# A decoder block on one core: the third and fourth group of 512 hidden columns computed as one more Strassen block

## The chip, the cores and the metric

The kernel runs as one program on 1 core of a Trainium2 chip. The metric is the device time of one execution in microseconds (us). Of several timed executions the median is given; the trace comes from one profiled execution and is read with times from the start of its span.

## The reference, cut to what matters

One decoder layer on x (512 positions, width 2048, float32): an attention half and a recurrent half behind one input projection, an output projection, and then the feed-forward part, which is all that the change concerns:

```
h2 = rms_norm(x, norm2_w) * (1 + scale2) + shift2
ff = square(relu(h2 @ w_ff1)) @ w_ff2          # w_ff1 2048 x 8192, w_ff2 8192 x 2048
x  = x + gate2 * ff
```

Everything is float32. A product of two float32 matrices is made of three TensorE products: each operand is split into a rounded high part and the rest (hi and lo), and hi*hi, hi*lo and lo*hi are added up in PSUM.

## The kernel before, in words

The 8192 hidden columns are 16 groups of 512 (`NG`). The first `PLAIN` = 4 groups are computed plainly, one after the other, by `hidden(g)` (the first of them by `first_hidden`, which also finishes the normalisation). A plain group takes 16 steps of 128 rows of `w_ff1`; each step loads a piece of the weight (`wraw`, L192), casts it to `whi` on ScalarE (L39), takes `wlo` on VectorE (L40) and runs 4 column blocks x 3 matmuls of 128x512 (`ch_mm`, L209 to L211): 192 matmuls a group. The result stands with channels in the partitions, as the second product wants it.

The other 12 groups are computed two at a time, as 6 blocks of 1024 columns, by Strassen's scheme with 7 half-size products instead of 8. A product (`product`, L1183) goes through four pieces of the contraction, u = 0 to 3, 12 matmuls each, so 48 a product and 336 a block. The result of a block has positions in the partitions, so it is turned by TensorE (`turn`, L1225), 32 transposes of 128x128 a block, in two halves.

What a product needs:

- **Weights.** 16 raw pieces a block (`raw`, L1155, 512 KB each, issued by SyncE). VectorE makes the sums and differences that products 5, 6, 7 and 4 want in place (L1163); ScalarE casts each piece to `vhi` (L1179), VectorE takes `vlo` (L1180). A product has its own piece 0, 1, 2, 3 of both.
- **Inputs.** Products 4 and 2 use the halves of h2 that are in SBUF. Products 1, 3, 5, 6 and 7 read the *forms* of h2 (sums of its quarters, hi and lo) from DRAM tensors `h_hid` and `h_lod`: for each half of the contraction (u = 0, 1 and u = 2, 3) one load of `Fh` and one of `Fl` (L1141, 512 KB each, issued by GpSimdE's queue, POOL). Four buffers of each kind exist.

The forms are made once, by `input_forms(u)` for u = 0 to 3: VectorE forms the four sums in `xf` (L1080 to L1083), then two casts to a staging tile `part` on ScalarE and two remainders on VectorE (L1042, L1043) are written to DRAM by POOL (L1046). There are 5 staging tiles and one `xf`, shared with `make_forms`, which does the same for each finished hidden group (`f_hid`, `f_lod`, the operands of the second product). These four generators are put into `tasks` behind group 0 and advanced by one step at each of 12 places of `hidden(1)` (`tick`, L1017), so all of them are recorded within group 1. Groups 2 and 3 then find the list empty.

The first Strassen block takes its products in the order 1, 3, 5, 6, 7, 4, 2; the others in 1, 5, 6, 7, 3, 4, 2. Products 1 and 5 of a block are copied from PSUM to SBUF on ScalarE (L1238).

The order of TensorE's work is the order of the program (manual schedule); the order on the other engines and queues is made by a scheduler when the kernel is built. Each queue then works strictly in that order: an instruction that waits holds up all behind it on its engine.

The part of the program that steps from the plain groups to the blocks:

```
for item, following in zip(items, items[1:] + [None]):
    ...
    call = part_of(following) if following else None
    if stage_ == 1:
        banks, ahead = product(i, hparts, 0, ws, "bg" if first and j < 2 else "mm", False, call)
```

`items` begins with block `PLAIN // 2`, and `call` makes the weight pieces of the following product while the present one runs.

Of the kernel before, what the change touches and what calls it, by code (L numbers as in the profile page):

```python
# [44 lines left out]
def hybrid_block(ctx, tc, x, c, positions, norm1_w, w_ada, b_ada, w_in, q_norm_w, k_norm_w,  # L45
# [922 lines left out]
    def first_hidden():  # L968

        banks = [bank("f1") for _ in range(4)]  # L970
        accs = [gv.tile([P, 512], F32, name="acc") for _ in range(2)]
        rbc = gv.tile([P, 512], F32, name="rbc", bufs=1)
        raws = []
        for k0 in range(0, NK, 2):
            for j, (whi, wlo) in enumerate(load_w(ff1_v, k0, 0, 512, None, raws=raws)):
                k = k0 + j
                if k >= 12:
                    h2[k] = pair(k)
                    split_to(h2[k], uT[k])
                ch_mm(banks, *h2[k], whi, wlo, k == 0, k == NK - 1)  # L980
                if k < 2:
                    dve.tensor_scalar(accs[k], raws[j], s2c[:, k:k + 1], None, op0=ALU.mult)
                else:
                    dve.scalar_tensor_tensor(accs[k % 2], raws[j], s2c[:, k:k + 1], accs[k % 2], op0=ALU.mult, op1=ALU.add)
                if 2 <= k < 8:
                    tick()
                if k == 8:
                    pr = bank("prow", tag="mm")
                    for ti in range(NT):
                        pe.transpose(pr[:, ti * P:(ti + 1) * P], r2[:, ti:ti + 1].broadcast_to([P, P]), ident)  # L990
                    act.copy(rbc, pr)
                if k >= 8:
                    for i in range((k - 8) * 2, (k - 8) * 2 + 2):
                        if i <= k:
                            h2_finish(i, rbc)
        bias = sm2
        run_all(to_cols(accs, bias))
        for j in range(4):
            r = xr.tile([P, 512], F32, name="relu", tag="x")
            dve.tensor_tensor(r, banks[j], rbc, op=ALU.mult)  # L1000
            act.activation(r, r, AF.Relu, bias=bias[:, j:j + 1])
            yield r
# [7 lines left out]
    def hidden(g):  # L1010
        banks = [bank("f1", tag="mm" if g % 2 else "bg") for _ in range(4)]
        for k0 in range(0, NK, 2):
            for j, (whi, wlo) in enumerate(load_w(ff1_v, k0, g * 512)):
                k = k0 + j
                ch_mm(banks, *h2[k], whi, wlo, k == 0, k == NK - 1)
                if 2 <= k < 14:
                    tick()  # L1017
        for j in range(4):
            r = xr.tile([P, 512], F32, name="relu", tag="x")
            act.activation(r, banks[j], AF.Relu)  # L1020
            yield r
# [4 lines left out]

    NG = FF // 512
    FORMS = 7
    PLAIN = 4
    KG = 4  # L1030

    def forms_in_dram(name, n, forms=FORMS):
# [59 lines left out]
    st_ = ctx.enter_context(ExitStack())  # L1092
    for g in range(PLAIN):
        rs = list(hidden(g) if g else first_hidden())
# [51 lines left out]
    def weights(view, g0, c0, order):  # L1146


        w = {}
        second = ((1, 1), (0, 1)) if order[1] == 3 else ((0, 1), (1, 1))  # L1150
        with tc.high_priority():
            for e, n in ((0, 0), *second, (1, 0)):
                for u in range(KG):
                    w[u, e, n] = raw = pools[f"raw{e + 1}{n + 1}"].tile([P, 2, 512], F32, name="raw2")
                    nc.sync.dma_start(raw, view[:, g0 + u, e, :, c0 + n * 512:c0 + (n + 1) * 512])  # L1155
        return w
# [161 lines left out]
    def part_of(item):  # L1318

        stage_, blk, j, i = item  # L1320
        if j == 0:
            part_of.w = weights(ff1_s, 0, blk * 1024, order_of(item)) if stage_ == 1 else \
                weights(ff2_s, blk[1] * KG, blk[0] * 1024, order)
        w, first = part_of.w, blk == PLAIN // 2

# [5 lines left out]
    def order_of(item):  # L1331
        return first_order if item[1] == PLAIN // 2 else order

    items = [(1, b, j, i) for b in range(PLAIN // 2, NG // 2) for j, i in enumerate(order_of((1, b)))]
    items += [(2, (q, c), j, i) for q in range(2) for c in range(NC) for j, i in enumerate(order)]
# [5 lines left out]
    for item, following in zip(items, items[1:] + [None]):  # L1341
        stage_, blk, j, i = item
        first = blk == PLAIN // 2
        if j == 0 and stage_ == 1 and not first:
# [75 lines left out]
def _program(arrays):  # L1420
    import concourse.bacc as bacc
    nc = bacc.Bacc("TRN2", target_bir_lowering=False, num_devices=1)
    args = [nc.dram_tensor(n, a.shape, mybir.dt.from_np(a.dtype), kind="ExternalInput").ap()
            for n, a in arrays.items()]
    args.append(nc.dram_tensor("out_0_dram", _OUTS[0][0], F32, kind="ExternalOutput").ap())
    with tile.TileContext(nc, schedule_with_timeline_sim=True) as tc:
        hybrid_block(tc, *args)
    return nc
# [10 lines left out]
```

## Time and profile before

| | |
|---|---|
| median of 3 runs | 2274.7 us (2272.88 to 2276.16) |
| profiled execution | 2273.89 us, span 2272.1 us |
| granted TensorE clock | 0.998 of full |
| TensorE matmul | 2219.7 us, 98% of the span |
| VectorE | 1809.6 us, 80% |
| ScalarE | 1097.3 us, 48% |
| GpSimdE | 441.8 us, 19% |
| DMA | 598.32 MB, mean 263 GB/s |

In the rows of the profile, PE is TensorE's matmul, PEld its weight load, DVE is VectorE, ACT ScalarE, POOL GpSimdE (its rows here are DMA issues), SP SyncE. A row names the line, the engine, the operation and `out<-in`. An interval in brackets is idle time just before the instruction and what ended it. Matmuls are pipelined: one lasts 0.39 us, but the next starts 0.227 us after it.

### The profile page before, as it was taken

The numbers are of one execution on the slowest core, as the hardware profiler recorded it, in microseconds if no ns is written. First come the engines' busy times: TensorE is split into PE (matmuls) and PEld (weight loads), VectorE is DVE, ScalarE is ACT, GpSimd is POOL, SyncE is SP. The second block draws the span as 40 slices with busy tenths as digits, with TensorE's granted clock in tenths as the row PEclk, the third lists the DMA queues.
The fourth block names the chain that finished last, engine by engine and source line by source line (L and its number), as shares of the span: only waits on it lengthen the run. The fifth ranks groups of instructions, "written<-read, shape, count | busy, mean of one in ns | idle before, by whom it ended". The sixth has DMA issues, their size and how long they took to land.

```text
span 2272.1 us, 33110 instructions
## 1 busy us (share of the span) xinstructions
PE 2219.7 (98%) x11769; PEld 1821.1 (80%) x11769; DVE 1809.6 (80%) x2765; ACT 1097.3 (48%) x1950; POOL 441.8 (19%) x664
## 2 busy tenths in 40 slices
PE   4899999999999999999999999999999999999999
PEld 3788778888778888888887888888888888888887
DVE  6999878768786575678658988998897779967878
ACT  5555434443454464457544555565564333443332
POOL 1000022000220000003232323323232222222221
PEclk9999999999999999999999999999999999999999
DMA  9799454646555266747879789879889987998884
GB/s 324 255 335 336 139 177 150 214 149 211 170 178 160 71 227 202 267 120 264 322 280 361 274 306 385 297 290 377 319 294 378 358 310 263 349 347 310 305 295 164
DMA packets 262583, 598.32 MB, mean 263 GB/s; under 512 B 23220, under 2 KB 43968, under 8 KB 262416
## 3 DMA queue, kind: packets, MB, share of 16 engines
q1 hardware_dynamic: 186800, 332.54, 43.6%
q0 software_dynamic: 70720, 254.21, 30.4%
q10 hardware_dynamic: 4896, 9.44, 1.2%
q8 instruction: 93, 1.52, 0.3%
q14 instruction: 74, 0.61, 0.1%
HBM read 518.49 MB, written 77.61 MB: 262 GB/s over the span
## 4 chain that ended last, share of the span: by engine, by line
PE 70%; DMA 10%; DVE 8%; issue 8%; POOL 2%; ACT 1%; SPq 0%; POOLq 0%; DVEq 0%; ACTq 0%
PE f L1197 9%; PE f L1196 9%; PE f L1195 9%; PE prj L201 8%; PE prj L203 8%; PE prj L202 8%; DMA araw<-in_w_ada_dram 3%; PE f L211 2%; PE f L209 2%; PE f L210 2%; DVE vlo L1180 2%; DMA f_lod<-fs 2%; DVE raw L1163 2%; PE prj L209 1%; PE prj L210 1%
## 5 line engine op out<-in xcount | busy, mean ns | idle before, releaser
L1179 ACT CAST vhi<-raw 128x1024 fp32r<-128x1024 f32 x392 | 413.5, 1055 | 534.1 <-PE f L1197 419.4
L1180 DVE TENSOR_TENSOR vlo<-raw,vhi 128x1024 fp32r<-128x1024 f32 x392 | 476.3, 1221 | 150.8 <-ACT vhi L1179 150.0
L1196 PE MATMUL f<-vlo,Fh 128*128 128x512 f32 x1376 | 537.1, 390 | 3.4 <-DVE vlo L1180 3.3
L1197 PE MATMUL f<-vhi,Fl 128*128 128x512 f32 x1376 | 535.8, 389 | 0.5 <-DMA Fl<-f_lod 0.5
L1195 PE MATMUL f<-vhi,Fh 128*128 128x512 f32 x1376 | 536.1, 390 | 0.0
L39 ACT CAST whi<-wraw 128x512 fp32r<-128x512 f32 (+1 forms) x368 | 219.8, 601 | 445.9 <-PE prj L203 309.7
L201 PE MATMUL prj<-whi,hi 128*128 128x512 f32 x896 | 363.5, 406 | 1.3 <-ACT gg L711 1.3
L203 PE MATMUL prj<-whi,lo 128*128 128x512 f32 x896 | 350.6, 391 | 0.0
L202 PE MATMUL prj<-wlo,hi 128*128 128x512 f32 x896 | 350.0, 391 | 0.6 <-DVE wlo L40 0.6
L40 DVE TENSOR_TENSOR wlo<-wraw,whi 128x512 fp32r<-128x512 f32 (+1 forms) x368 | 243.3, 666 | 115.3 <-ACT whi L39 109.5
L131 DVE SCALAR_TENSOR_TENSOR acc<-araw,sc,acc 128x512 f32<-128x512 f32 (+1 forms) x392 | 254.0, 674 | 99.8 <-DMA araw<-in_w_ada_dram 98.6
L1196 PEld LDWEIGHTS f<-vlo,Fh 128*128 128x128 f32 x1376 | 258.3, 188 | 62.3 <-DVE vlo L1180 8.9
L1197 PEld LDWEIGHTS f<-vhi,Fl 128*128 128x128 f32 x1376 | 258.3, 188 | 54.2 <-DMA Fl<-f_lod 0.9
L1195 PEld LDWEIGHTS f<-vhi,Fh 128*128 128x128 f32 x1376 | 258.3, 188 | 53.7
L1163 DVE TENSOR_TENSOR raw<-raw,raw 128x1024 f32<-128x1024 f32 x224 | 268.3, 1218 | 3.5 <-DMA raw<-in_w_ff_dram 3.1
L203 PEld LDWEIGHTS prj<-whi,lo 128*128 128x128 f32 x896 | 168.1, 188 | 36.6 <-DVE lo L243 0.3
L201 PEld LDWEIGHTS prj<-whi,hi 128*128 128x128 f32 x896 | 168.3, 188 | 36.4 <-ACT gg L711 1.6
L202 PEld LDWEIGHTS prj<-wlo,hi 128*128 128x128 f32 x896 | 168.6, 188 | 33.5 <-DVE wlo L40 1.7
L1141 POOL DMA_DIRECT2D Fh<-f_hid x112 | 79.0, 705 | 424.0 <-PE f L1197 410.3
L211 PE MATMUL f<-hi,wlo 128*128 128x512 f32 x256 | 99.9, 390 | 1.2 <-DVE wlo L40 1.2
L209 PE MATMUL f<-hi,whi 128*128 128x512 f32 x256 | 100.3, 392 | 0.0
L210 PE MATMUL f<-lo,whi 128*128 128x512 f32 x256 | 99.6, 389 | 0.0
(311 smaller groups left out, 2912.0 us busy)
## 6 DMA issues: line engine op xcount, KB each, us to landing
raw<-in_w_ff_dram SPq DMA_DIRECT2D x224, 512.0 KB, 10.1
araw<-in_w_ada_dram SPq DMA_DIRECT2D x384, 256.0 KB, 4.3
Fh<-f_hid POOLq DMA_DIRECT2D x112, 512.0 KB, 6.7
Fl<-f_lod POOLq DMA_DIRECT2D x112, 512.0 KB, 7.8
wraw<-in_w_in_dram SPq DMA_DIRECT2D x104, 512.0 KB, 4.4
Fh<-h_hid POOLq DMA_DIRECT2D x60, 512.0 KB, 6.4
Fl<-h_lod POOLq DMA_DIRECT2D x60, 512.0 KB, 7.4
f_hid<-part POOLq DMA_DIRECT2D x48, 512.0 KB, 8.0
```

What stands on the lines that cost most here:

```text
L39: nc.scalar.copy(hi, src)
L40: (eng or nc.vector).tensor_tensor(lo, src, hi.bitcast(F32), op=ALU.subtract)
L131: dve.scalar_tensor_tensor(acc, raw[:, k - k0], vec[:, k:k + 1], acc, op0=ALU.mult, op1=ALU.add)
L201: pe.matmul(banks[ti], lhsT=hi[:, ts], rhs=whi, start=first, stop=False)
L202: pe.matmul(banks[ti], lhsT=hi[:, ts], rhs=wlo, start=False, stop=False)
L203: pe.matmul(banks[ti], lhsT=lo[:, ts], rhs=whi, start=False, stop=last)
L1163: dve.tensor_tensor(dst, a, b, op=ALU.subtract)
L1179: cast_done.append(act.copy(hi, src))
L1180: split_done.append(dve.tensor_tensor(lo, src, hi.bitcast(F32), op=ALU.subtract))
L1195: pe.matmul(banks[t], lhsT=fh[u][a][:, ts], rhs=whi[:, a], start=first, stop=False)
L1196: pe.matmul(banks[t], lhsT=fh[u][a][:, ts], rhs=wlo[:, a], start=False, stop=False)
L1197: pe.matmul(banks[t], lhsT=fl[u][a][:, ts], rhs=whi[:, a], start=False, stop=end)
```

## The change

One number changes:

```
@@ -1026,7 +1026,7 @@
     NG = FF // 512
     FORMS = 7
-    PLAIN = 4
+    PLAIN = 2
     KG = 4
```

The loop over plain groups ends after groups 0 and 1. `items` begins at block 1 instead of block 2, so there are 7 Strassen blocks, and the *first* block (order 1, 3, 5, 6, 7, 4, 2) now follows group 1 directly. The making of the forms stays in `hidden(1)`.

The scheduler orders the queues anew. In the following lists the number behind a name tells buffers apart.

**POOL, from the end of the forms of u = 1 on.** `part_11234` and `part_11235` are the second pair of forms (slots 6 and 7) of u = 1, `part_11287` to `part_11316` belong to u = 2, `part_11368` to `part_11387` to u = 3. Before:

```order
L1046 DMA h_hid_10581<-part_11234 128x2x512
L1046 DMA h_lod_10582<-part_11217 128x2x512
L1046 DMA h_lod_10582<-part_11235 128x2x512
L1046 DMA h_hid_10581<-part_11287 128x2x512
L1046 DMA h_lod_10582<-part_11288 128x2x512
L1046 DMA h_hid_10581<-part_11315 128x2x512
L1046 DMA h_lod_10582<-part_11316 128x2x512
L1046 DMA h_hid_10581<-part_11368 128x2x512
L1046 DMA h_lod_10582<-part_11369 128x2x512
L1046 DMA h_hid_10581<-part_11386 128x2x512
```

Now the loads of product 1 (`Fh_11572` to `Fl_11578`) and the first one of product 3 (`Fh_11648`) stand among them:

```order
L1046 DMA h_lod_10582<-part_11235 128x2x512
L1141 DMA Fh_11572<-h_hid_10581 128x2x512
L1141 DMA Fl_11574<-h_lod_10582 128x2x512
L1141 DMA Fh_11576<-h_hid_10581 128x2x512
L1141 DMA Fl_11578<-h_lod_10582 128x2x512
L1141 DMA Fh_11648<-h_hid_10581 128x2x512
L1046 DMA h_hid_10581<-part_11287 128x2x512
L1046 DMA h_lod_10582<-part_11288 128x2x512
L1046 DMA h_hid_10581<-part_11315 128x2x512
L1141 DMA Fl_11650<-h_lod_10582 128x2x512
L1046 DMA h_lod_10582<-part_11316 128x2x512
L1046 DMA h_hid_10581<-part_11368 128x2x512
```

The loads of the first block have moved from behind all writes of forms to a place between them; the writes of u = 2 and 3 stand behind the loads of product 1.

**POOL, the inputs of products 1 and 3.** Before, the first block's loads stood together: `Fh_12206` to `Fl_12212` for product 1, `Fh_12282` to `Fl_12288` for product 3.

```order
L1141 DMA Fh_12206<-h_hid_10581 128x2x512
L1141 DMA Fl_12208<-h_lod_10582 128x2x512
L1141 DMA Fh_12210<-h_hid_10581 128x2x512
L1141 DMA Fl_12212<-h_lod_10582 128x2x512
L1141 DMA Fh_12282<-h_hid_10581 128x2x512
L1141 DMA Fl_12284<-h_lod_10582 128x2x512
L1141 DMA Fh_12286<-h_hid_10581 128x2x512
L1141 DMA Fl_12288<-h_lod_10582 128x2x512
```

Now the second half of product 3 is `Fh_11652` and `Fl_11654`; `Fh_11726` and `Fh_11730` belong to product 5, `Fh_11806` to product 6. `part_11443` and `part_11449` are forms of hidden group 1.

```order
L1046 DMA h_lod_10582<-part_11387 128x2x512
L1046 DMA f_hid_10579<-part_11443 128x2x512
L1046 DMA f_hid_10579<-part_11449 128x2x512
L1141 DMA Fh_11652<-h_hid_10581 128x2x512
L1141 DMA Fh_11726<-h_hid_10581 128x2x512
L1141 DMA Fh_11730<-h_hid_10581 128x2x512
L1141 DMA Fh_11806<-h_hid_10581 128x2x512
L1141 DMA Fl_11654<-h_lod_10582 128x2x512
```

The second half of product 3 is loaded behind the write of two forms of group 1 and behind three loads of later products.

**ACT, where product 1 passes into product 3.** Before, `vhi_12200` is the last weight piece of product 1, `vhi_12226`, `vhi_12242`, `vhi_12258` and `vhi_12276` are the pieces of product 3, `s10` and `s11` take product 1 out of PSUM.

```order
L1179 CAST vhi_12226<-raw2_12164 128x1024
L1042 CAST part_12077<-fs_12068 128x1024
L1042 CAST part_12083<-fs_12068 128x1024
L1179 CAST vhi_12242<-raw2_12166 128x1024
L1042 CAST part_12089<-fs_12068 128x1024
L1179 CAST vhi_12258<-raw2_12168 128x1024
L1238 COPY s10_12115<-f2_12204 128x512
L1179 CAST vhi_12276<-raw2_12170 128x1024
L1238 COPY s11_12116<-f2_12205 128x512
```

Now `vhi_11558` and `vhi_11562` are pieces 1 and 2 of product 1, `vhi_11592` to `vhi_11642` the four pieces of product 3, `vhi_11669` is piece 0 of product 5:

```order
L1042 CAST part_11368<-xf_11333 128x1024
L1179 CAST vhi_11558<-raw2_11524 128x1024
L1179 CAST vhi_11562<-raw2_11526 128x1024
L1042 CAST part_11386<-xf_11333 128x1024
L1238 COPY s10_11481<-f2_11570 128x512
L1238 COPY s11_11482<-f2_11571 128x512
L1179 CAST vhi_11592<-raw2_11530 128x1024
L1179 CAST vhi_11608<-raw2_11532 128x1024
L1179 CAST vhi_11624<-raw2_11534 128x1024
L1179 CAST vhi_11642<-raw2_11536 128x1024
L1042 CAST part_11443<-fs_11434 128x1024
L1179 CAST vhi_11669<-raw2_11522 128x1024
```

Both copies of product 1 now stand ahead of all four casts of product 3, and two of product 1's own pieces stand behind a cast of the last form of u = 3.

More of the change, by code (lines that the diff above doesn't have):

```diff
@@ L1028, in hybrid_block @@
     FORMS = 7
-    PLAIN = 4
+    PLAIN = 2
     KG = 4
```

## The prediction

> **What bounds the kernel now.** I read the page first, then the busy time by stretches around the change, then TensorE's timeline at the seam between the plain groups and the first block, then the queues there.
>
> ```profile
> PE 2219.7 (98%) x11769; PEld 1821.1 (80%) x11769; DVE 1809.6 (80%) x2765; ACT 1097.3 (48%) x1950; POOL 441.8 (19%) x664
> PE 70%; DMA 10%; DVE 8%; issue 8%; POOL 2%; ACT 1%; SPq 0%; POOLq 0%; DVEq 0%; ACTq 0%
> ```
>
> TensorE is busy for 98% of the span and carries 70% of the chain that ended last. So matmuls saved are time saved, and idle TensorE is time lost, one for one. The next four rows are, in order, the three plain groups 1 to 3, the first Strassen block, and two later blocks (from one block's product 2 to the next block's). Columns: length of the stretch, then busy time and instructions of PE, PEld, DVE, ACT, POOL, then the granted clock, the DMA share and GB/s.
>
> ```profile
> 1038.76:1169.43 130.67, 130.67 (x579) 108.19 (x578) 78.91 (x123) 67.98 (x112) 34.18 (x51) 1.00 0.83 296
> 1169.43:1249.42 79.99, 78.93 (x354) 64.55 (x352) 69.02 (x70) 44.30 (x51) 24.50 (x36) 1.00 0.97 355
> 1307.53:1388.28 80.75, 80.40 (x370) 66.31 (x368) 71.98 (x75) 45.41 (x52) 25.23 (x37) 1.00 0.87 324
> 1388.28:1469.01 80.73, 80.38 (x369) 66.31 (x368) 71.99 (x75) 45.41 (x52) 24.66 (x37) 1.00 0.88 327
> ```
>
> TensorE never waits in the plain groups: 576 matmuls in 130.67 us, one each 0.227 us. In the blocks it hardly does, but DVE is at 72 of 81 us there, against 79 of 131. At the seam:
>
> ```profile
> 1169.21 0.39 PE L211 MATMUL f<-hi,wlo 128*128 128x512 f32 x1
> 1169.43 0.39 PE L1195 MATMUL f<-vhi,Fh 128*128 128x512 f32 x1
> 1318.41 1.91 PE L1225 MATMUL pt<-ident,s 128*128 128x128 f32 x16
> 1320.08 0.48 PE L1195 MATMUL f<-vhi,hi 128*128 128x512 f32 x1
> ```
>
> The first two rows: the last plain matmul and the first one of the block follow each other in 0.22 us, so the seam costs nothing now. The other two: 16 transposes take 1.67 us.
>
> **The saving.** Two plain groups cost 130.67 x 2/3 = 87.1 us. A block in the steady state costs 80.7 us. That is 6.4 us less. The count agrees: 384 - 336 = 48 matmuls x 0.227 = 10.9 us less, 32 transposes at 1.67 / 16 = 3.3 us more, and 1.2 us of small waits that each steady block has. The added 20 input loads, 16 differences on DVE and turning lie beside matmuls in the steady blocks, which have them too; so they are in the 80.7. All blocks behind the first only shift.
>
> **What covered the seam, and what is left of it.** Groups 2 and 3 were also the cover behind which the forms of h2 were finished and the first block's operands fetched. POOL's queue in the timeline:
>
> ```profile
> 1079.78 1.42 POOL L1046 DMA_DIRECT2D h_lod<-part  x2
> 1095.30 0.71 POOL L1046 DMA_DIRECT2D h_hid<-part  x1 [4.19 <-ACT part L1042]
> 1098.67 0.71 POOL L1046 DMA_DIRECT2D h_hid<-part  x1 [1.26 <-ACT part L1042]
> 1101.32 0.71 POOL L1046 DMA_DIRECT2D h_lod<-part  x1
> 1143.05 0.72 POOL L1141 DMA_DIRECT2D Fh<-h_hid  x1
> 1167.17 0.72 POOL L1141 DMA_DIRECT2D Fl<-h_lod  x1 [12.95 <-PE f L211]
> ```
>
> The DMA view, with the median from issue to landing: first the writes of forms and the block's raw weights issued from 1076 to 1104 us, then the block's loads from 1167 to 1170 us.
>
> ```profile
> h_hid<-part POOLq DMA_DIRECT2D x6, 512.0 KB, 6.0
> h_lod<-part POOLq DMA_DIRECT2D x6, 512.0 KB, 7.2
> raw<-in_w_ff_dram SPq DMA_DIRECT2D x4, 512.0 KB, 11.3
> ...
> Fl<-h_lod POOLq DMA_DIRECT2D x3, 512.0 KB, 5.7
> Fh<-h_hid POOLq DMA_DIRECT2D x2, 512.0 KB, 5.4
> ```
>
> Group 1 ends at 1038.76 + 130.67 / 3 = 1082.3 us. The last write of forms is issued at 1101.3, 19 us behind that; it did not matter, since the first load came at 1143 and the block at 1169. Now the block is due at 1082.3. The same work on DVE and ACT, and the prices that I use:
>
> ```profile
> 1091.22 0.42 DVE L1080 TENSOR_TENSOR xf<-u,u 128x256 f32<-128x256 f32 x1
> 1093.16 0.75 DVE L1082 TENSOR_TENSOR xf<-xf,u 128x256 f32<-128x256 f32 x2
> 1094.91 2.00 ACT L1179 CAST vhi<-raw 128x1024 fp32r<-128x1024 f32 x2
> 1096.32 2.35 DVE L1180 TENSOR_TENSOR vlo<-raw,vhi 128x1024 fp32r<-128x1024 f32 x2
> L1179 ACT CAST vhi<-raw 128x1024 fp32r<-128x1024 f32 x28 | 29.4, 1052 | 32.0 <-DVE raw L1163 15.5 <-PE f L1197 14.3 <-issue 1.1
> L1238 ACT COPY s<-f 128x512 f32<-128x512 f32 x4 | 2.3, 584 | 0.8 <-PE f L1197 0.8
> L1163 DVE TENSOR_TENSOR raw<-raw,raw 128x1024 f32<-128x1024 f32 x16 | 19.2, 1219 | 0.0
> ```
>
> A cast of 128x1024 takes 1.05 us, a remainder or difference 1.2, a copy out of PSUM 0.58, a POOL issue 0.71, a piece (12 matmuls) 2.72, a product 10.9.
>
> *Stall 1, product 1.* Its piece 1 is cast on ACT behind `part_11368`, the cast of a form of u = 3. That needs DVE's sums of u = 3 in the one `xf`, so DVE must be through with the remainders of u = 2, and the second of these needs a staging tile: the fifth tile back, freed when the write of `part_11217` lands. It was issued at 1079.8 (first of the two in the row), so it lands at 1087.0. From there: remainder 1.2, six sums 0.33 apart (the row of two) = 2.0, one weight remainder between them 1.2, so 1091.4; cast 1.05, piece 1's cast 1.05, on DVE its remainder 1.2: 1094.7. Piece 0 runs ahead of that, since `Fl_11574`, issued at about 1081.9, lands at 1087.6. Pieces 1 to 3 take 8.2 us: product 1 ends at 1102.9 instead of 1093.2, 9.7 us late.
>
> *Stall 2, product 1 to 3.* ACT holds both copies of product 1 ahead of product 3's first cast: 0.58 x 2 + 1.05, then a remainder 1.2: 3.4 us.
>
> *Stall 3, the middle of product 3.* From product 1's end ACT takes 1.2 (copies) + 4.2 (four casts) + 1.05 (`part_11443`) = 6.4; the cast of product 5's piece 0 waits for DVE: fourth remainder at 6.6, difference at 7.8; cast at 8.9, `part_11449` at 9.9. Only then does POOL issue that tile's write, `Fh_11652`, three more loads and, sixth, `Fl_11654`: 9.9 + 5 x 0.71 = 13.5, landing 5.7 later at 19.2. Product 3's first half was done at 3.4 + 5.4 = 8.8. TensorE waits 10.4 us.
>
> *The clock.* Ahead of 94.43 us TensorE sat idle for 4 us; the second row is the busy time from 93 to 99 us:
>
> ```profile
> 94.43 2.08 PE L209 MATMUL prj<-hi,whi 128*128 128x512 f32 x4 [4.06 <-ACT hi L339]
> 93.00:99.00 6.00, 4.57 (x10) 3.33 (x11) 6.00 (x14) 4.26 (x8) 0.00 (x0) 0.50 0.40 144
> ```
>
> The granted clock was 0.50: 10 matmuls took 4.57 us, 2.3 more than 10 x 0.227. Behind stall 3 I add 2.3; behind stall 1 the slow stretch falls into piece 0, which has room. The Trainium skill ("TensorE: Matmul & The Clock Gate", section "Part 1: The HAM clock gate (the "warmup" mystery)") says that the clock halves after an idle window of about 3.4 us and is full again after a busy one; by that a stall costs 1.7 us on top, where the row has 2.3, and the sum would be 0.6 lower.
>
> *The sum.* -6.4 + 9.7 + 3.4 + 10.4 + 2.3 = +19.4. On the profiled execution, 2273.9 us (span 2272.1 and 1.8 around it), that is 2293.3; this execution lies 0.8 below the median of 2274.7, so **2294.1**.
>
> The stalls aren't in the trace of before, so they are bounded. Low: stall 1 only by product 1's input, 1081.9 + 5.4 + 10.9 - 1093.2 = 5.0; stall 2 only until the first cast, 2.2; stall 3 only by POOL's order, in which `Fh_11806`, waiting for the buffer of product 3's first half, stands ahead of `Fl_11654`: 0.71 + 5.4 = 6.1; no slow clock. Together 13.3, so +6.9: 2281.6. High: landings of 11.3 us, as the raw weights had beside the writes, add 4.1 and 5.6; slow clock behind stall 1 too, 2.3: 37.8, so +31.4: 2306.1. Below nothing is excluded, since the order puts each wait on TensorE's only work. I take the middle prices because the medians are those of the same DMAs at the same place. The Trainium skill ("DMA: Bandwidth & Descriptors", section "Anatomy of one DMA — SWDGE (gpsimd) path") gives 2 us and size by 436 GB/s, an estimate of 3.2 us for 512 KB; by that the landings of stalls 1 and 3 would be 4.0 and 2.5 shorter and the sum 6.5 lower; the trace, with 5.4 to 7.2, does not agree.
>
> **The rivals.**
>
> - *The cover holds (faster).* TensorE starts the block at once and only the 6.4 us show: 2268.3. It decides at the seam: all forms in DRAM and loaded by 1093. For it: DVE has 52 us of idle time in the three plain groups, and two of product 1's pieces were cast at 1094.9, far ahead. Against: writes at 1098.7 and 1101.3, and POOL's order, which now puts loads ahead of these writes. 6%.
> - *Stall and gain cancel.* About 6 us of stalls: 2275. This, or a change that does not do what it says, though the order has 48 matmuls less: 4%.
> - *Product 3's input comes in time.* Stalls 1 and 2 alone: 9.7 + 3.4 - 6.4 = +6.7, 2281.4. It needs ACT's casts to be earlier than POOL's turn. 12%.
> - *DVE becomes the bound of the first block.* It has 69 of 80 us there; the sums and remainders of u = 2 and 3 (16 sums at 0.33 and 8 remainders at 1.2, 15 us) now partly fall into it. If half of it, 8 us, comes on top: 2302. 12%.
>
> The forecast keeps 66%. The low end 2280 takes in the third rival and the low bounds; the high end 2305 the fourth and most of the high bounds. About 0.2%, 4.5 us, is what a measurement of this kernel can tell from none: faster 0.06, same 0.04, slower 0.90.
>
> **What the changed profile would show.** Right: a steady block of 80.7 us; between 1082 and about 1135 us three idle stretches of TensorE, the first until about 1087 with a second one inside product 1, about 3 us ahead of product 3 with ACT's `vhi` as what ended it, about 10 us in its middle ended by the landing of `Fl`; matmuls 0.43 us apart behind the long one; PE's busy time 5 to 8 us less (10.9 - 3.3, and the slow clock against it). Wrong: no idle row over 2 us at the seam, a long one at another product, or the steady blocks slower than 80.7 us.

## The result, and the profile after

The changed kernel takes 2297.9 us (median of 6 runs, 2295.6 to 2302.0), the kernel before 2274.5 us beside it (6 runs, 2272.6 to 2281.3). The ratio is 1.0104, with a 95% interval of 1.0094 to 1.0114: 23.5 us slower, where 2294.1 was forecast, in a range of 2280 to 2305.

The page of the profiled execution (2295.6 us, span 2293.9), with TensorE's busy time, the chain that ended last and the two groups of matmuls whose idle time ends by loaded inputs:

```profile
PE 2220.1 (97%) x11753; PEld 1820.3 (79%) x11753; DVE 1848.4 (81%) x2791; ACT 1108.6 (48%) x1946; POOL 457.6 (20%) x684
PE 70%; issue 12%; DMA 8%; DVE 5%; POOL 3%; ACT 1%; SPq 0%; POOLq 0%; DVEq 0%; ACTq 0%
L1195 PE MATMUL f<-vhi,Fh 128*128 128x512 f32 x1456 | 570.3, 392 | 19.1 <-DMA Fh<-h_hid 17.5
L1197 PE MATMUL f<-vhi,Fl 128*128 128x512 f32 x1456 | 569.6, 391 | 5.5 <-DMA Fl<-h_lod 4.7
```

The last number group of a row is idle time of TensorE ahead of these instructions. 24.6 us stand there, 22.2 of them behind loads of forms. TensorE is busy 2220.1 us, as long as before (2219.7), although the program has 48 matmuls less and 32 short transposes more, which the prediction's prices put at 7.6 us less (10.9 - 3.3).

The busy time by stretches, with the columns of the prediction: group 1, the first Strassen block, a later block.

```profile
1036.78:1080.42 43.64, 43.64 (x195) 35.95 (x193) 34.09 (x59) 25.80 (x46) 14.08 (x22) 1.00 0.88 308
1080.42:1191.39 110.97, 86.35 (x353) 69.32 (x353) 79.76 (x88) 51.80 (x60) 33.64 (x49) 0.86 0.90 340
1248.60:1329.35 80.75, 80.40 (x370) 66.33 (x368) 71.99 (x75) 45.41 (x52) 24.97 (x36) 1.00 0.87 326
```

A later block takes 80.7 us, as it did before. The first block takes 111.0 where it took 80.0. Its clock is 0.86 of full, and 24.6 of its 111.0 us are idle. Where, TensorE's timeline shows (the last plain matmul, then every row of the seam that has an idle time):

```profile
1080.19 0.39 PE L211 MATMUL f<-hi,wlo 128*128 128x512 f32 x1
...
1090.69 0.79 PE L1195 MATMUL f<-vhi,Fh 128*128 128x512 f32 x1 [10.11 <-DMA Fh<-h_hid]
...
1092.50 0.79 PE L1197 MATMUL f<-vhi,Fl 128*128 128x512 f32 x1 [0.59 <-DMA Fl<-h_lod]
...
1107.41 0.49 PE L1195 MATMUL f<-vhi,Fh 128*128 128x512 f32 x1 [1.62 <-ACT vhi L1179]
1108.67 0.79 PE L1196 MATMUL f<-vlo,Fh 128*128 128x512 f32 x1 [0.77 <-DVE vlo L1180]
...
1122.95 0.77 PE L1195 MATMUL f<-vhi,Fh 128*128 128x512 f32 x1 [7.38 <-DMA Fh<-h_hid]
...
1128.30 0.80 PE L1197 MATMUL f<-vhi,Fl 128*128 128x512 f32 x1 [4.16 <-DMA Fl<-h_lod]
```

These are the three stalls: 10.7 us ahead of and inside product 1, 2.4 as product 1 passes into product 3, 11.5 in the middle of product 3. Product 5 begins at 1135.23. Without a wait it would have begun 96 matmuls behind 1080.42, at 1102.2. So the seam loses 33.0 us: 24.6 idle, and 8.4 in which TensorE worked more slowly. About 7.0 of these are half clock (an estimate: the three stretches in the last section have 14.9 us of matmuls, which start 0.427 us apart instead of 0.227); the rest is lost around the waits. From product 5's first matmul to the first of the third block it takes 3.0 us less than in the kernel before (136.9 for 139.9). Most of it is time that TensorE waits for VectorE: 2.5 us in that stretch of the kernel before (1.5 for a `vlo`, 1.0 for sums ahead of transposes), 0.4 in the changed kernel.

The DMA view from 1076 to 1084 us has for each queue the packets, MB and share of the 16 engines' time (q1 is that of SP's loads, q0 POOL's), and then the issues with the median us to landing:

```profile
q1 hardware_dynamic: 842, 1.63, 62.2%
q0 software_dynamic: 307, 1.14, 34.9%
issues: line engine op xcount, KB each, median us to landing
raw<-in_w_ff_dram SPq DMA_DIRECT2D x3, 512.0 KB, 13.9
...
Fh<-h_hid POOLq DMA_DIRECT2D x2, 512.0 KB, 12.1
Fl<-h_lod POOLq DMA_DIRECT2D x2, 512.0 KB, 13.0
```

Product 1's four loads land 12 to 13 us after their issue (medians of two each), where 5.4 and 5.7 were the prices in the prediction. Five loads of raw weights left SP from 1073.9 us on, just ahead of them (three count in this view), and SP's queue has most of the engines' time.

**How the runs are compared.** In every trace I read, on TensorE's timeline, when each product of the first block begins, counted from the start of the last plain matmul (which lies between 1079.1 and 1082.7 us in the runs with two plain groups), and when the third block of the program begins. The third block's start measures the whole seam: it is 161.9 us behind in the kernel before and 191.9 in the changed one. The difference, 30.0, less the 6.4 that a block saves, is 23.6; the medians differ by 23.5. The first-block order is 1, 3, 5, ... but for the last four versions with 1, 2, 5, ... (marked *).

| run | 1st product | 2nd | 3rd | third block | median us | ratio to the kernel before, 95% |
|---|---|---|---|---|---|---|
| before | 0.2 | 11.1 | 22.0 | 161.9 | 2274.5 | |
| changed | 10.5 | 27.2 | 55.0 | 191.9 | 2297.9 | 1.0094 to 1.0114 |
| product 1 from SBUF | 0.2 | 27.5 | 51.8 | 188.7 | 2293.3 | 1.0070 to 1.0100 |
| products 1 and 3 from SBUF | 0.2 | 27.6 | 38.5 | 181.2 | 2286.7 | 1.0039 to 1.0072 |
| matmuls in the gaps | 12.3 | 25.4 | 54.2 | 191.1 | 2294.5 | 1.0076 to 1.0106 |
| raw loads behind | 10.9 | 26.2 | 54.8 | 191.7 | 2296.8 | 1.0085 to 1.0115 |
| exchange in SBUF | 7.3 | 24.2 | 52.2 | 189.0 | 2294.2 | 1.0075 to 1.0108 |
| exchange, product 1 from SBUF | 0.2 | 22.6 | 46.9 | 183.8 | 2290.2 | 1.0055 to 1.0085 |
| forms first | 7.5 | 21.1 | 36.3 | 192.0 | 2296.3 | 1.0086 to 1.0116 |
| four plain groups, late forms | 10.0 | 23.8 | 42.7 | 179.5 | 2289.4 | 1.0052 to 1.0086 |
| products 1, 2 first, forms first * | 0.2 | 15.4 | 26.3 | 177.9 | 2283.6 | 1.0028 to 1.0058 |
| products 1, 2 first * | 0.2 | 27.3 | 38.2 | 181.3 | 2287.1 | 1.0042 to 1.0072 |
| ... other layout * | 0.2 | 14.1 | 25.0 | 180.8 | 2283.5 | 1.0026 to 1.0054 |
| ... product 5's sums early * | 0.2 | 15.9 | 26.8 | 179.4 | 2285.1 | 1.0025 to 1.0053 |

### The profile page after: what moved, and what is told of

The parts are those of the page before. It is cut to its first block, busy times and chain, and to the rows that moved or that the text cites. A ratio compares the mean times of both kernels' runs of the same rounds, so it can differ in the third digit from the quotient of the medians.

```text
span 2293.9 us, 33146 instructions
## 1 busy us (share of the span) xinstructions
PE 2220.1 (97%) x11753; PEld 1820.3 (79%) x11753; DVE 1848.4 (81%) x2791; ACT 1108.6 (48%) x1946; POOL 457.6 (20%) x684
## 4 chain that ended last, share of the span: by engine, by line
PE 70%; issue 12%; DMA 8%; DVE 5%; POOL 3%; ACT 1%; SPq 0%; POOLq 0%; DVEq 0%; ACTq 0%
PE f L1196 9%; PE f L1197 9%; PE f L1195 9%; PE prj L201 9%; PE prj L203 9%; PE prj L202 9%; DMA f_lod<-fs 2%; DMA Fl<-h_lod 2%; PE prj L210 2%; PE prj L211 2%; PE prj L209 2%; DVE vlo L1180 1%; DMA Fl<-f_lod 1%; PE f L211 1%; PE f L210 1%
## 5 line engine op out<-in xcount | busy, mean ns | idle before, releaser
L1179 ACT CAST vhi<-raw 128x1024 fp32r<-128x1024 f32 x420 | 442.9, 1056 | 571.6 <-PE f L1197 460.3
L1180 DVE TENSOR_TENSOR vlo<-raw,vhi 128x1024 fp32r<-128x1024 f32 x420 | 510.9, 1221 | 162.9 <-ACT vhi L1179 161.9
L1195 PE MATMUL f<-vhi,Fh 128*128 128x512 f32 x1456 | 570.3, 392 | 19.1 <-DMA Fh<-h_hid 17.5
L1197 PE MATMUL f<-vhi,Fl 128*128 128x512 f32 x1456 | 569.6, 391 | 5.5 <-DMA Fl<-h_lod 4.7
L1196 PE MATMUL f<-vlo,Fh 128*128 128x512 f32 x1456 | 571.0, 392 | 3.4 <-DVE vlo L1180 3.4
L39 ACT CAST whi<-wraw 128x512 fp32r<-128x512 f32 (+1 forms) x336 | 199.8, 599 | 404.6 <-PE prj L203 304.1
L1195 PEld LDWEIGHTS f<-vhi,Fh 128*128 128x128 f32 x1456 | 275.0, 189 | 77.4 <-DMA Fh<-h_hid 10.5
L40 DVE TENSOR_TENSOR wlo<-wraw,whi 128x512 fp32r<-128x512 f32 (+1 forms) x336 | 221.7, 665 | 81.5 <-ACT whi L39 80.7
L1141 POOL DMA_DIRECT2D Fh<-h_hid x70 | 49.4, 707 | 204.9 <-PE f L1197 194.3
L1195 PE MATMUL f<-vhi,hi 128*128 128x512 f32 x224 | 87.7, 392 | 0.0
L1197 PE MATMUL f<-vhi,lo 128*128 128x512 f32 x224 | 87.2, 389 | 0.0
```

The costliest lines, as they stand in the source:

```text
L39: nc.scalar.copy(hi, src)
L40: (eng or nc.vector).tensor_tensor(lo, src, hi.bitcast(F32), op=ALU.subtract)
L1179: cast_done.append(act.copy(hi, src))
L1180: split_done.append(dve.tensor_tensor(lo, src, hi.bitcast(F32), op=ALU.subtract))
L1195: pe.matmul(banks[t], lhsT=fh[u][a][:, ts], rhs=whi[:, a], start=first, stop=False)
L1196: pe.matmul(banks[t], lhsT=fh[u][a][:, ts], rhs=wlo[:, a], start=False, stop=False)
```

## The experiments

**1. Product 1 without its loads.** My theory for stall 1 was the chain of casts on ACT; the trace after shows the landing of loads as what ended it. In this run product 1 reads halves of h2 that lie in SBUF, so it computes another product with the same work.

```
-        if src is hparts and i in (4, 2):
+        calls.append(i)
+        if src is hparts and (i in (4, 2) or len(calls) <= 1):
```

> Product 1 of the first block reads halves of h2 that lie in SBUF (those of product 4 or 2, so another product is computed); its four 512 KB loads are gone, all else stands. Theory A (my step for stall 1: the cast of piece 1 behind the form of u = 3 on ACT is the bound, the slow loads only hid it): product 1 starts by 1083 us on the changed kernel's axis, but its piece 1 still waits until about 1095.5, it ends at about 1103.7 instead of 1105.6, and the run takes 2294 to 2297 us. Rival B (the landing of the loads at 1090.6 to 1095.6 is the whole of stall 1): product 1 ends by 1093, 12 us earlier, and the run takes 2284 to 2288 us.

Measured: 2293.3 us. Product 1 starts at once, but its second piece waits. TensorE's timeline, the two rows of product 1 with an idle time:

```profile
1095.43 0.80 PE L1198 MATMUL f<-vhi,hi 128*128 128x512 f32 x1 [11.28 <-ACT vhi L1182]
1098.16 0.80 PE L1199 MATMUL f<-vlo,hi 128*128 128x512 f32 x1 [1.93 <-DVE vlo L1183]
```

And ACT's, a cast of the last form and the casts of pieces 1 and 2 behind it:

```profile
1093.39 1.04 ACT L1042 CAST part<-xf 128x1024 fp32r<-128x1024 f32 x1 [1.03 <-DVE xf L1082]
1094.34 1.99 ACT L1182 CAST vhi<-raw 128x1024 fp32r<-128x1024 f32 x2
```

The second product begins at 27.5, as in the changed kernel (27.2). Without the loads nothing of stall 1 is gone: theory A's mechanism holds, and B, which the row of the trace after suggests, falls. A's numbers don't hold: product 1 ends 4 us later than it said, and the run lies 0.7 below its range. Part of that is a shift of the chain itself, as DVE's remainder for piece 1 ends 17.1 us behind the last plain matmul here and 15.3 in the changed kernel. The 3.2 us that the run does gain come at the third product (51.8 for 55.0); I put them down to POOL's queue, which has four transfers less.

**2. Product 3 without its loads too.**

```
-        if src is hparts and i in (4, 2):
+        calls.append(i)
+        if src is hparts and (i in (4, 2) or len(calls) <= 2):
```

> Products 1 and 3 of the first block read halves of h2 that lie in SBUF (other products are computed); eight loads are gone, the forms are made and written as before. Theory (stall 3 is the wait for product 3's input behind the writes in POOL's queue): no idle stretch over 2 us in the middle of product 3, that is 11.5 us of idle time and the second long stretch of half clock, about 3 us, less than in the run with product 1 alone: 2278 to 2284 us. Rival (the forms are late for any reader: the third product, 5, takes over the wait): 2288 to 2294 us, with the long idle stretch now inside or ahead of product 5.

Measured: 2286.7 us, between the two ranges; 6.6 less than with product 1 alone. TensorE's waits from 1079 to 1170 us (total, times, longest):

```profile
PE f L1198 <- ACT vhi L1182: 11.4, 1, 11.4
PE f L1199 <- DVE vlo L1183: 5.5, 4, 1.9
```

Product 3 takes 10.9 us, with no wait: stall 3 was the wait for its loads. Of the 13.3 us that it gives back at the third product (38.5 for 51.8 in the run before), 5.8 go again up to the third block, most of them in products 5 and 6, where DVE's remainders are now what comes last (three of the four waits for `vlo`, 3.6 us; the longest, 1.9, lies in product 1). The theory names the right cause and promised too much.

**3. Full clock in the gaps.**

```
+                if src is hparts and len(warmed) < 3 and (i, u) == ((1, 0), (3, 0), (3, 2))[len(warmed)]:
+                    warm((44, 6, 48)[len(warmed)])
                 mm(u, *ws[u], range(2))
```

`warm(n)` issues n matmuls of tiles of h2 into a PSUM bank that nobody reads.

> 98 matmuls that nobody reads are put where TensorE sits idle: 44 ahead of product 1, 6 ahead of product 3, 48 in its middle (10.0, 1.4 and 10.9 us at 0.227 each, a little less than the idle stretches). Theory (half clock costs 7 us: matmuls 0.427 us apart for some 30 of them, in three stretches, against the 2.3 that I forecast): no half-clock stretch over 4 us between 1080 and 1140, run 5 to 8 us shorter than the changed kernel: 2290 to 2293 us. Rival (the slow matmuls lie beside waits that would last as long anyway, or the idle time grows by as much): within 2 us of the changed kernel, 2296 to 2299 us.

Measured: 2294.5 us, 3.4 below the changed kernel, with intervals that overlap; in the trace the third block starts 0.8 earlier. The rows of the two long runs of added matmuls, and the longest wait left in product 3:

```profile
1081.21 10.31 PE L1189 MATMUL warm<-hi,hi 128*128 128x512 f32 x44 [1.76 <-ACT relu L1020]
...
1110.87 11.04 PE L1189 MATMUL warm<-hi,hi 128*128 128x512 f32 x48
...
1125.45 0.80 PE L1205 MATMUL f<-vhi,Fl 128*128 128x512 f32 x1 [3.09 <-DMA Fl<-h_lod]
```

Product 1 runs at full clock: it takes 13.1 us up to product 3's start instead of 16.7. But it starts 1.8 later, for the first added matmul had to wait 1.8 us for its bank, and product 3's second half still waits for `Fl`. The theory's 5 to 8 us did not come, and the time lies between its range and the rival's. Of the 7.0 us of half clock about 2.7 are left (5.73 us of matmuls from 1124.35 to 1131.18, by the same working). The other 4.3 lay largely beside inputs that are late anyway, so taking them away is worth 1 to 3 us. The experiment is not clean, since one half-clock stretch of 6.8 us remains and the added matmuls delay product 1 themselves.

**4. Raw weights behind the loads.**

```
+                behind = order is first_order and (e, n) != (0, 0)
...
+                    with tc.issue_after(loads[3].ins) if behind else ExitStack():
```

> The eight raw weight loads of the first block that product 1 does not need (4 MB, issued up to 1076.7 us in the changed kernel) are issued only after product 1's input loads. Theory (the loads land 11 us after issue because 4.5 MB stand ahead of them in the DMA engines at 417 GB/s, 2.5 of them raw weights): product 1's loads land 5 to 7 us after issue, product 1 ends 3 to 6 us earlier, the run takes 2291 to 2295 us. Rival (landing depends on the queue of POOL's own transfers, not on what SP issues): landing 10 to 11 us after issue, 2297 to 2299 us. A third outcome, slower than 2300 us, would say that product 3's or 5's weights are then late.

Measured: 2296.8 us, and it tells nothing of the theory. The edit orders the queues when the kernel is built, but puts no wait on SP: the five loads left at 1075.6, as in the changed kernel at 1073.9. In the DMA view from 1076 to 1084 us SP's queue has even more of the engines' time, and the loads land later:

```profile
q1 hardware_dynamic: 955, 1.86, 75.1%
q0 software_dynamic: 184, 0.68, 20.9%
...
Fh<-h_hid POOLq DMA_DIRECT2D x2, 512.0 KB, 12.4
Fl<-h_lod POOLq DMA_DIRECT2D x2, 512.0 KB, 13.3
```

How much sooner the loads would land without SP's stays open.

**5 and 6. The casts off the chain.** First alone, then with product 1 from SBUF.

```
-    ... ("raw12", 4), ("spl3", 1), ("s15", 1), ("raw22", 4), ("spl1", 1), ("spl2", 1), ("s67", 1), ...
+    ... ("raw12", 4), ("spl3", 1), ("s15", 1), ("spl1", 1), ("spl2", 1), ("raw22", 4), ("s67", 1), ...
```

> Two entries of the list that lays out SBUF for the blocks change places: the split weights of pieces 1 and 2 now lie over the first eight tiles of uT (forms u = 0, 1), and the raw weights of product 3 over the last eight (u = 2, 3). So the casts of product 1's pieces no longer wait for the sums of u = 3; the loads of product 1 stand. Theory (stall 1 has two causes that end within 2 us of each other, the cast chain and the landing of the loads; removing one leaves the other): product 1 ends 0 to 2.5 us earlier, 2295 to 2298 us. Rival (the cast chain alone is the cause): product 1 ends by 1097, 2286 to 2290 us.

> Both causes of stall 1 are removed: the exchange in the list of the run before, and product 1 reads halves of h2 in SBUF (another product is computed). Theory: product 1 runs through from 1080.4 and ends by 1092.5, 13 us earlier than in the changed kernel, without half clock; the forms of u = 2 and 3 don't get earlier, so stall 3 grows by 3 to 8 us, and the run takes 2280 to 2288 us. Rival (all that stall 1 gives is given back in stall 3, because POOL's queue and not product 1 sets when product 3's input lands): 2291 to 2296 us.

Measured: 2294.2 and 2290.2 us, each between the ranges of its theory and its rival. The second product begins 3.0 earlier in the first (24.2), 4.6 in the second (22.6). TensorE's waits in the second:

```profile
PE f L1198 <- ACT vhi L1182: 6.2, 1, 6.2
PE f L1198 <- DMA Fh<-h_hid: 5.2, 1, 5.2
PE f L1200 <- DMA Fl<-h_lod: 4.9, 1, 4.9
PE f L1199 <- DVE vlo L1183: 2.2, 1, 2.2
```

Neither theory came in full. The tiles are free earlier, but ACT's queue still has the casts of two of product 1's pieces (from 1090.91) behind a cast of the last form (1089.96), so 8.4 us of stall 1 (6.2 + 2.2) remain even without loads. Nothing of what is gained ahead of the second product is lost again in stall 3: the third product begins 8.1 earlier than in the changed kernel, and the third block too. That the gain would be given back is ruled out.

**7. The forms of h2 ahead of those of group 0.**

```
-                    tick()
+                    tick(2)
...
-        for _ in make_forms(fs, fparts, g, plain_stage):
-            pass
         if g == 0:
             tasks.extend(input_forms(u) for u in range(KG))
+        tasks.append(make_forms(fs, fparts, g, plain_stage))
...
```

> As the changed kernel, but the forms of h2 are made before the forms of group 0's output, and two steps of them per k-tile of group 1 instead of one. Theory (the forms are late because their staging tiles wait for the landing of 3.5 MB of group 0's writes, issued from 1055 to 1064 us): the last write of a form of h2 is issued by 1090 instead of 1102.2; stalls 1 and 3 shrink, 2284 to 2291 us. Rival (the DMA engines are full at 417 GB/s from 1080 to 1106 us whatever the order, so that the loads of products 1 and 3 land as late): 2295 to 2300 us.

Measured: 2296.3 us. The last form is issued at 1089.0 instead of 1102.2, as the theory has it, and the third product begins at 36.3 instead of 55.0. Yet the third block starts where it did. The wait has moved, to product 4, the sixth of the block:

```profile
1162.90 0.79 PE L1199 MATMUL f<-vhi,hi 128*128 128x512 f32 x1 [11.40 <-ACT vhi L1183]
1166.09 0.79 PE L1200 MATMUL f<-vlo,hi 128*128 128x512 f32 x1 [2.40 <-DVE vlo L1184]
```

Product 4's raw weights are issued at 1143 to 1146 us, with a median of 19.6 us to landing, and DVE's first difference of them starts at 1160.46, when one lands. I put the late issue down to the forms of groups 0 and 1, which are made later now, so that the SBUF under them comes free late. The time lies in the rival's range, but neither theory had that.

**8. The cover alone.** The kernel before, with the forms started in group 3.

```
-        if g == 0:
+        if g == 2:
             tasks.extend(input_forms(u) for u in range(KG))
```

> The kernel before, four plain groups, but with the forms of h2 started in group 3 instead of group 1: the same lateness at the seam as in the changed kernel, without the work that it saves. Theory (what the change costs is the lost cover alone): the seam shows the same stretches, about 10, 2.4 and 11.5 us idle and two or three of half clock, 31 to 33 us in all, and the run takes 2303 to 2309 us; the changed kernel lies 6.4 below it. Rival (part of the loss comes with the shorter plain stage itself, weights and forms in the same 87 us): 2285 to 2298 us.

Measured: 2289.4 us, 15.3 above the kernel before; the theory's 2303 is missed, the rival's range met. TensorE's waits at the seam:

```profile
PE f L1195 <- DMA Fh<-h_hid: 10.2, 2, 9.6
PE f L1197 <- DMA Fl<-h_lod: 5.2, 1, 5.2
```

And POOL's timeline, a load of product 1 and, behind it, the last form's write of h2 (the last plain matmul starts at 1167.26):

```profile
1169.71 0.72 POOL L1141 DMA_DIRECT2D Fh<-h_hid  x1
...
1177.69 0.72 POOL L1046 DMA_DIRECT2D h_lod<-part  x1 [0.42 <-DVE fs L1051]
```

So a lost cover alone, with all work as before, makes the same first and third stall: up to product 5 the seam loses 20.7 us (42.7 for 22.0), of 33.0 in the changed kernel. It is less, since the forms were not as late: the last is issued 10.4 us behind the plain groups, in the changed kernel 22.0 (1102.2 against 1080.2). The DMA engines had hardly more room. SP's row of raw weights, the stretch of group 3, and POOL's first write of a form of h2:

```profile
1136.80 21.88 SPq L1155 DMA_DIRECT2D raw<-in_w_ff_dram  x8
...
1123.70:1167.26 43.56, 43.56 (x194) 36.04 (x193) 29.09 (x49) 19.88 (x29) 13.95 (x20) 1.00 0.83 308
...
1141.68 0.71 POOL L1046 DMA_DIRECT2D h_hid<-part  x1 [0.57 <-ACT part L1042]
```

Eight raw weight loads leave in group 3, and its DMA share is 0.83, against 0.88 in group 1 of the changed kernel. What differs is when the forms start: the first write leaves 25.6 us ahead of the last plain matmul, in the changed kernel 15.2 (1065.0), both times next behind the forms of the group before. These 10.4 us are most of the 11.6 by which the last write is less late. Why the forms of group 2 are written sooner in the next group than those of group 0 is open. My expectation had taken the lateness for given by the group in which the forms start; the rival's reason, weights and forms in the same 87 us, is not shown either.

**9 to 12. Cover from other products.** Product 2 needs no form, and product 1's input still lies in SBUF (the even tiles of h2). In these four versions the first block takes the order 1, 2, 5, 6, 7, 3, 4.

```
-    first_order = (1, 3, 5, 6, 7, 4, 2)
+    first_order = (1, 2, 5, 6, 7, 3, 4)
...
+        if src is hparts and i == 1 and "fp" not in pools:
+            return [[[h2[4 * u + 2 * a][j][:, 256:512] for a in range(2)] for u in range(KG)] for j in range(2)]
...
+            if "fp" not in pools:
+                ph0.close()
+                pool_of("fp", 4)
```

With it comes a layout in which early things lie over what is free early, and the edit of experiment 7:

> A version that computes the reference: the forms first as in the run before; the first block begins with product 1 read from the even tiles of h2 in SBUF and product 2 from the odd ones, in the order 1, 2, 5, 6, 7, 3, 4 with product 2's result held in PSUM until product 6; the operand buffers are opened only behind product 1; and the list that lays out SBUF puts what is needed early over what is free early. So no load is needed in the first 21.8 us of the block. Theory (the whole loss is the missing cover of the forms): no idle stretch over 2 us up to product 5 and less than 5 us of idle time in the block, 2268 to 2275 us, at or below the kernel before. Rival (the DMA backlog still makes product 5 or 6 wait): 2276 to 2284 us, with one idle stretch of 5 to 12 us ended by the landing of Fl.

Measured: 2283.6 us, 14.3 below the changed kernel and 9.7 above the kernel before: the rival's range, but not its mechanism, since no wait of TensorE at the seam ends with a load. The third product begins 4.3 us behind that of the kernel before, where it was 33.0. Without experiment 7's edit:

> The reordered first block of the run before (1, 2, 5, 6, 7, 3, 4; products 1 and 2 read from SBUF), but with the forms of h2 made behind those of group 0's output, as in the changed kernel. Theory (21.8 us of cover do most of it, the order of the forms little): the relu tiles and the raw weights behind them come free 15 us earlier than with the forms first, so product 6 waits less; product 5's second half waits up to 5 us for its input instead; 2275 to 2285 us. Rival (the forms' place in the queue decides): the last form is written at about 1100, product 5 waits 8 us or more, 2286 to 2292 us.

Measured: 2287.1 us, in the rival's range. Here the order of the forms does decide, but at product 1 (10.3 us behind ACT's casts), not at product 5. In the better of the two, products 6 and 7 wait. TensorE's waits there:

```profile
PE f L1204 <- DVE vlo L1188: 5.6, 4, 2.9
PE f L1203 <- DVE s L1248: 4.8, 1, 4.8
PE f L1203 <- ACT vhi L1187: 1.7, 2, 1.2
```

Two tries at these waits, by layout alone:

> As the version with the forms first and the order 1, 2, 5, 6, 7, 3, 4, with another layout of SBUF: only the last of product 6's four raw weight tiles (b22) lies over the relu tiles, instead of two, and the split weights of pieces 1 and 2 of product 1 over tiles that are free by 1076. Theory (what is left of the loss in that version is product 6's weights, which were issued at 1108 to 1110 us behind the relu tiles, so that DVE's differences bunched up from 1114 to 1137 and product 3 waited too): three of the four loads are issued before 1100, product 6 starts without a wait, and the run takes 2272 to 2279 us. Rival (the bunching comes from DVE's work itself, remainders of group 1's forms beside two sets of differences): the waits at product 6, 7 and 3 stay, 2280 to 2285 us.

Measured: 2283.5 us, in the rival's range. Three of the four loads still left SP at 1108 to 1110 us, as one that waits for a relu tile stood ahead of the others in SP's queue, so the theory's condition was not made. The wait named `DVE s`, now 6.1 us, stands ahead of product 7. It ends with DVE's first addition of product 6's result (1142.4), which comes behind ACT's four copies (1138 to 1140) and a wait of 1.25 us for a write of forms. The last version moves both the loads and the copies forward; pieces of its list:

```
-("raw22", 4), ("s15", 1), ("fs2", 1),
-("stA", 3), ("stB", 1), ("s67", 1),
...
+("raw22", 3), ("raw22l", 1), ("s5", 1),
+("fs2", 1), ("stA", 3), ("stB", 1), ("s7", 1), ("s6", 1), ("s1", 1),
```

> As the version before it, with two things moved in SBUF: the accumulators of product 5 lie over relu tiles, which are free from 1108, instead of over the squares of group 1, which are not free until 1127 to 1138; and three of the four raw weight tiles of b22 have a pool of their own, so that their loads no longer stand in SP's queue behind the one that waits for a relu tile. Theory (the two waits of the versions with order 1, 2, 5, 6, 7, 3, 4 are product 6's weights, loaded at 1108, and product 7's PSUM banks, which product 5's late copy holds until 1139): the three loads are issued before 1100, the copies of product 5 stand before 1120, the idle stretches of 3.7, 2.6 and 6.1 us at products 6 and 7 shrink to under 4 in all with their half clock, and the run takes 2269 to 2276 us, level with the kernel before or below it. Rival (the DVE remainders and staging tiles of group 1's forms bind there anyway): 2277 to 2283 us.

Measured: 2285.1 us, no gain, and above the ranges of theory and rival. The loads now left by 1082 us and the copies at 1122 to 1124; the condition is met but for 4 us. The busy time in the middle of the seam says why it doesn't help (the third number group behind the length is DVE's):

```profile
1099.70:1139.60 39.90, 32.41 (x131) 25.12 (x131) 39.77 (x38) 18.53 (x22) 14.80 (x22) 0.94 0.94 337
```

DVE is busy for 39.8 of 39.9 us, and 8.9 of TensorE's 13.3 us of waits at the seam end with its work (`vlo` 5.8, `s` 3.1). With the loads out of the way DVE is what is late: the prediction's fourth rival, which holds here, and not in the changed kernel, where DVE was busy for 79.8 of 111.0. No version beats the kernel before.

## Why the prediction was right, and which terms were off

- *The saving, 6.4: right.* Two groups took 87.1; a steady block takes 80.7, and the third block's start agrees with the medians only when these 6.4 are taken off (23.6 and 23.5 us).
- *Stall 1, 9.7 for product 1's end: the mechanism right, later by 3.0 at product 3's start* (27.2 behind the last plain matmul, where 0.2 + 10.9 + 9.7 + 3.4 = 24.2 was forecast). I had put a cast of the last form on ACT ahead of piece 1's cast, and it is: experiment 1 shows that this chain alone makes a stall of the same size. The step that failed is the price of a landing. DVE waited for a staging tile whose write (issued at 1077.26) I let land after 7.2 us; it took 10.0, where the same write of the kernel before took 6.0. The DMA view at its issue, then DVE's timeline:

```profile
h_lod<-part POOLq DMA_DIRECT2D x1, 512.0 KB, 10.0
...
1087.37 1.23 DVE L1043 TENSOR_TENSOR part<-xf,part 128x1024 fp32r<-128x1024 f32 x1 [2.65 <-DMA h_lod<-part]
...
1094.27 1.22 DVE L1180 TENSOR_TENSOR vlo<-raw,vhi 128x1024 fp32r<-128x1024 f32 x1
```

  On this axis, which is 2.0 us earlier than that of before, I had the first DVE row at 1085.0 and the end of the second at 1092.7; it ended at 1095.5. And the first two loads, which I took to land after 5.4 to 5.7 us and so well ahead of that chain, landed 11.0 and 12.1 after issue (the second at 1092.5), so that the trace names them for a wait that had two ends within some 3 us. That there would be a short wait ahead of product 1 and a longer one behind its piece 0 was wrong for that reason: there is one of 10.1, and 0.6 in piece 0.
- *Stall 2, 3.4: the mechanism right, 1.0 shorter*: 1.6 + 0.8 = 2.4, ended by `vhi` and `vlo` as said.
- *Stall 3, 10.4: right, 11.5*, in two parts: 7.4 until `Fh_11652` has landed and, two matmuls later, 4.2 until `Fl_11654` has. POOL's queue is as worked out:

```profile
1111.44 0.71 POOL L1046 DMA_DIRECT2D f_hid<-part  x1 [8.50 <-ACT part L1042]
1115.57 0.72 POOL L1046 DMA_DIRECT2D f_hid<-part  x1 [3.42 <-ACT part L1042]
1116.28 2.83 POOL L1141 DMA_DIRECT2D Fh<-h_hid  x4
1119.11 2.11 POOL L1141 DMA_DIRECT2D Fl<-h_lod  x3
```

  `Fl_11654`, the first of the three, leaves 13.5 us behind product 1's end (1105.64), the 13.5 of the forecast. It lands after 9.1 us (1128.25) instead of 5.7: the same term is short, by 3.4.
- *The clock, 2.3: far too small as a sum, and it isn't a term to add.* Half clock took about 7.0 us, in three stretches and not one; but in experiment 3, with 4.3 of them gone, the inputs hold TensorE up nearly as long. The step that failed is that I priced it once, behind stall 3, and let the slow stretch behind stall 1 fall into spare time: product 1 takes 16.7 us up to product 3's start there.
- *The sum.* 33.0 us were lost at the seam for 25.8 forecast: 3.0 more up to product 3 and 4.2 more from there to product 5, both mostly by landings of 9 to 12 us where I took 5.4 to 7.2. The prediction had these as its high bound (11.3 us, "as the raw weights had beside the writes"); with it the seam would have come to 35.5 (25.8 + 4.1 + 5.6). It chose the medians of the same DMAs "at the same place". The loads were not at the same place: those whose medians I took came 66 us behind the last write of a form (1167.2 against 1101.3). The write was, but there the raw weights of the block left SP at 1095, and here from 1073.9 on, ahead of it; that this is why it landed late is argued, not shown. The 3.0 us that two blocks take less behind product 5 was in no step. It brings the forecast nearer than its terms were, and that is luck.
- *PE's busy time, 5 to 8 less: wrong*, 0.4 more, since matmuls at half clock count as busy for longer, by 7.0 us and not by 2.3.
- *The rivals.* That the cover holds, or product 3's input is in time: the rows of stalls 1 and 3 rule it out. That stalls and gain cancel: the seam lost 33.0, not 6. DVE as the bound: not here, but next in line (experiment 12).

The Trainium skill ("DMA: Bandwidth & Descriptors", section "Anatomy of one DMA — SWDGE (gpsimd) path") was cited for 2 us and size by 436 GB/s, an estimate of 3.2 us for a load. The landings of 9.1 to 13.0 us here are three to four times that; from 1084.40 to 1098.05 us the core moved 408 GB/s (the row stands in the last section), near the rate that the section states. What the estimate leaves out, I take it, is the queue ahead.

## What to carry to other kernels

Before a stage with no idle time is shortened, ask what is finished behind it for the next one, and set how far that work already reaches past its end (here 19 us in the trace of before) against the time saved (6.4). If several queues are to be emptied at once at the new place, price a transfer also from the fullest stretch of the trace, and not only from where it came with little beside it; here 11.3 was nearer to the 10.0 and 9.1 measured than 7.2 and 5.7. The engine that a wait is put down to is only the last of those that were late: taking away the loads that ended the wait of 10.1 us left the second product where it was (27.5 for 27.2), so an experiment that removes one input tells more than the row.

## What the runs showed of the hardware

**Half clock behind idle stretches.** The granted clock is the column ahead of the DMA share. Rows of the changed kernel, stretch by stretch:

```profile
1084.40:1098.05 13.65, 6.78 (x15) 4.89 (x16) 10.14 (x17) 8.47 (x12) 4.99 (x7) 0.50 1.03 408
...
1108.29:1111.70 3.41, 3.02 (x7) 2.45 (x8) 3.41 (x4) 2.85 (x4) 0.26 (x1) 0.50 0.00 0
1118.53:1132.18 13.65, 5.07 (x11) 3.65 (x12) 10.53 (x10) 0.62 (x1) 6.85 (x10) 0.50 0.97 344
```

All lengths are multiples of 3.41 us, and matmuls in them start 0.427 us apart. The Trainium skill ("TensorE: Matmul & The Clock Gate", section "Part 1: The HAM clock gate (the "warmup" mystery)") gives a window of 3413 ns, half clock behind an idle window and full clock behind a busy one. The window's length agrees. But the second row's stretch follows a window in which TensorE was idle for 2.0 us only (1.62 and the first 0.39 of 0.77), and the first row's did not end behind the window of 1091.2 to 1094.6, in which it was idle for 0.59. In experiment 2, 1.53 us of idle time in one window (1123.56 to 1126.97) left the clock full. So 2.0 us of waits in one window already cost clock here, and 0.59 us in the recovery prolonged it.

**Two queues on full DMA engines.** From 1076 to 1084 us (the rows in the first section) SP's few weight loads had 62% of the engines' time and POOL's queue, with eight transfers issued, 35%. So a few weight loads took most of the engines' time beside a longer queue of writes and loads that others wait for. That they held it up, and that holding them back would help, is not shown, as experiment 4 did not hold them back; no run looked for another cause of the late landings either.
